# Convolution tiles by group, state steps beside the last convolutions, and decode attention's products on VectorE

## The chip, the cores and the metric

The kernel runs on one core of one Trainium2 chip. The core has TensorE (PE, with its weight loads PEld), VectorE (DVE), ScalarE (ACT), GpSimd (POOL) and SyncE (SP), which here only starts transfers. The metric is the device time of one execution in microseconds. Lower is better.

## What is computed

One step of a decoder of two layers, for a prompt of 1024 tokens and, with the same weights, 8 samples of one token each. All numbers are float32. The first layer (the "even" one) is the one that matters here. Its input projection gives attention's q, k, v and gate, the state-space part's gate z, and the channels xBC with their step dt. Attention's gated output and the state-space part's normalised output go through one output projection. Cut to what the change touches:

```
def even_layer(hn, ...):
    u = hn @ w_in
    q, k, v, g_att, z, xbc, dt_raw = split(u)
    o = dilated attention of the prompt, or, for the samples, of q over cached k, v
    att = o * silu(g_att)
    xbc, new_conv = causal_conv(xbc, conv_buf, conv_w, conv_b)   # 4 taps, then silu
    xs, bm, cm = split(xbc)          # 1024 channels x, 2 x 128 of B, 2 x 128 of C
    dt = softplus(dt_raw + dt_bias); a = -exp(a_log)
    y, new_state = ssd_scan(xs, dt, a, bm, cm, d_skip, ssd_state)
    y = rmsnorm(y * silu(z), ssd_norm_w)
    return concat(att, y) @ w_out

def ssd_scan(...):                   # chunks of 128 tokens, 2 groups of 8 heads
    acum = cumsum(dt * a)            # within a chunk
    decay = exp(acum_i - acum_j), lower triangle
    y_intra = (C B^T * decay * dt) x
    s_local = sum_j B_j exp(last - acum_j) dt_j x_j
    state  <- state * exp(last) + s_local          # from chunk to chunk
    y = y_intra + (C state_before) * exp(acum) + d_skip * x
```

Group 0 of the scan needs B and C of group 0 and channels 0 to 511 of x; group 1 needs the others. The second layer (mLSTM) follows and is not touched.

## The kernel before

**Layout.** Activations lie transposed: 128 channels on the partitions, 1032 tokens (1024 of the prompt, 8 samples) along the free dimension. A product in float32 is made of three reduced-precision products: each operand is split into a high and a low part (`split`, L89), and `mm3` (L103) adds high x high, high x low and low x high. A weight tile of 128 columns by 1024 rows comes with one load, is split by ScalarE (L90) and VectorE (L91), and `Weights` (L115) keeps one split tile ahead. `proj_c` multiplies it with one third of the tokens (344 columns, `c` = 0, 1, 2): 24 matmuls.

**Order of the work.** The program is written as one stream. The builder's scheduler takes that order as a priority: an engine whose next instruction is not ready by the scheduler's own reckoning gets a later one that is. What the engines run is a fixed order per engine, with waits. Tiles come from pools with a fixed number of buffers, and an instruction that writes a new tile waits until the pool has a free one: 15 slabs `S` of 128 x 1040, 3 buffers `EP`, 5 PSUM banks `X` and 3 `MM`, 4 `TMP`.

**First stages.** The input is normalised, and for four pairs of heads q, k, v are projected (to 274 us in the profile). Prompt attention is cut into small pieces in `attq`, which `att_pump` takes out beside the projections: `att_a` (scores; VectorE adds the mask and finds the maximum, L433; ScalarE takes the exponential, L434), `att_b` (VectorE scales P, L468; TensorE transposes it, pT, L470; it is copied, L473 and L475; TensorE multiplies it with v, pO, L487).

**Convolutions** (from 274 us). A loop over 12 weight tiles f: 0 to 7 are x, 8 and 9 are B of groups 0 and 1, 10 and 11 are C. Each has three `conv_c` (the projection; ScalarE copies it out, L242), then `conv_taps` (ScalarE's first tap, L248, and VectorE's three others, L250) and, one tile later, `conv_act` (ScalarE's tanh, L254, and VectorE, L255). Beside tiles 0 to 5 the rest of prompt attention is pumped; beside tiles 4 and later `dpump(1)`, three times per tile, takes a step of `dq`. `dt_prep` (the step sizes, cumulative sums and decays; it stores `acd`) is written behind tile 7.

**Decode attention** is the first part of `dq`: `dec_prep`, eight `dec_k`, `dec_soft`, eight `dec_v`, `dec_fin`. One `dec_k` loads 512 KB of cached keys into an `EP` buffer, POOL multiplies them with q (L634), and VectorE sums (L635). `dec_v` does the same with the values (L651, L652). `dec_fin2` (at gate tile 1) transposes the result on TensorE.

**Gate tiles.** A second loop over 12 weight tiles, `gate_c` each time: 0 to 7 are z, 8 to 11 attention's gate. Beside them run the 16 steps of the state scan, (chunk c, group g), in two halves. `ssd_prep` (`ssd_a`) loads a row of `acd` to all partitions, POOL masks it (L739), ScalarE takes exponentials (L741), TensorE makes C B^T and transposes B and x (pcb, pxt), VectorE multiplies (L747, L758, L759), and ScalarE copies B^T (sbt, L749). `ssd_main` (`ssd_b`) has the products py, pi and psl on TensorE, the state and the results on VectorE (L780 to L789), and one addition on POOL (L791). It runs one step behind the preparation. The order is all chunks, and in each both groups:

```
sq = deque((c, g) for c in range(8) for g in range(2))
own = f < 8 and (c < 2 or f < 2)
```

so tiles 0 and 1 take three steps each and the others two, after one step ahead of the loop. Once per gate tile `dpump` takes one step of the samples' own state update (`dss_step`), in which POOL's products (L839, L841) and VectorE's instructions (L840, L842) alternate. Behind tile 7, `mix_y` multiplies by the gate and normalises; TensorE sums squares there (pst, L188).

Of the kernel before, what the change touches and what calls it, by code (L numbers as in the profile page):

```python
# [28 lines left out]
def body(ctx, tc, I, O):  # L29
# [26 lines left out]
    def S(name, dt=F32):  # L56
        return slab.tile([128, 1040], dt, tag="S", name=name)
# [199 lines left out]
    def conv_raw(raw=None):  # L257
        raw = S("craw") if raw is None else raw
        G.memset(raw[:, 0:3], 0.0)
        return raw  # L260
# [250 lines left out]
    def att_pump(n, limit):  # L511
        for _ in range(n):
            if attq and attq[0][0] < limit:
                attq.popleft()[1]()
# [63 lines left out]
    cur["ep"] = pool("ep0", 3, wstack0)  # L578
    eap = pool("eap", 2, wstack0)

    wq0 = Weights([(I["wf"][f], 1024) for f in range(24)])


    dtb = C("dtb", [128, 16], I["dtb"].partition_broadcast(128))
# [45 lines left out]
    def dec_k(j):  # L630
        t = EP("dk")
        load(t[:, :1024], I["ck"][:, j * 1024 : j * 1024 + 1024])
        tv = t[:, :1024].rearrange("p (a b) -> p a b", b=64)
        G.tensor_tensor(tv, tv, q_b.unsqueeze(1).broadcast_to([128, 16, 64]), mult)  # L634
        V.reduce_sum(dsc[:, j * 16 : j * 16 + 16], tv, AX.X)  # L635

    def dec_soft():
# [9 lines left out]
    def dec_v(j):  # L647
        t = EP("dv")
        load(t[:, :1024], I["cv"][:, j * 1024 : j * 1024 + 1024])
        tv = t[:, :1024].rearrange("p (a b) -> p a b", b=128)  # L650
        G.tensor_tensor(tv, tv, dsc[:, 0:128].unsqueeze(1).broadcast_to([128, 8, 128]), mult)  # L651
        V.reduce_sum(dao[:, j * 8 : j * 8 + 8], tv, AX.X)  # L652

    def dec_fin():
# [39 lines left out]
    scs = C("scs", [128, 12, 3, 8], I["scs"])  # L694
    xbs = C("xbs", [128, 12, 8])
    cvo = C("cvo", [128, 12, 3])
    xbc = []
    later = deque()
    for f in range(12):
        w = wq0.next()  # L700
        raw = conv_raw()
        o = S("cout")
        for c in range(3):
            conv_c(w, xh, xl, c, raw, xbs[:, f])
            if c == 1 and later:
                later.popleft()()
            if f < 6:
                att_pump(3, 4)
            if f > 3:
                dpump(1)  # L710
        conv_taps(raw, o, scw[:, f], scb[:, f : f + 1], cvo[:, f])
        later.append(lambda raw=raw, o=o: conv_act(raw, o))
        xbc.append(o)
        if f == 5:
            att_pump(80, 4)
        if f == 7:
            dt_prep()
    later.popleft()()
    xy, bc = xbc[:8], xbc[8:]
    store(O["sconv"], cvo)  # L720


    st = C("ssdst", [128, 1040])
    ssd_state = {}

    def ssd_prep(c, g):
        tok = slice(c * 128, c * 128 + 128)
        g0 = c * 16 + g * 8
        E = EP("sE")[:, :1024]
        load(E, acd[g0 : g0 + 8, :].rearrange("h i -> (h i)").partition_broadcast(128))  # L730
        Ev = E.rearrange("p (h i) -> p h i", h=8)
        Bt, Ct = bc[g], bc[2 + g]
        ea = None
        if c > 0:
            ea = eap.tile([128, 520], F32, tag="ea", name="ea")[:, :512]
            for u in range(2):
                src = acd[g0 : g0 + 8, :].rearrange("(j u) i -> u j i", u=2)[u]
                load(ea[u * 64 : u * 64 + 64].rearrange("p (j i) -> p j i", j=4), src.partition_broadcast(64))
        G.affine_select(Ev, Ev, [[0, 8], [1, 128]], ALU.is_ge, -1e30, base=0, channel_multiplier=-1)  # L739
        for h in range(8):  # L740
            A.activation(Ev[:, h], Ev[:, h], AF.Exp, bias=nacum[:, g0 + h : g0 + h + 1])  # L741
        if c > 0:
            A.activation(ea, ea, AF.Exp)
        pc = X("pcb")
        PE.matmul(pc[:, 0:128], Bt[:, tok], Ct[:, tok], start=True, stop=True)
        PE.transpose(pc[:, 128:256], Bt[:, tok], ident)
        V.tensor_tensor(Ev, Ev, pc[:, 0:128].unsqueeze(1).broadcast_to([128, 8, 128]), mult)  # L747
        bt = SM("sbt", [128, 128])
        A.copy(bt, pc[:, 128:256])  # L749
        px = X("pxt")  # L750
        for j in range(4):
            PE.transpose(px[:, j * 128 : j * 128 + 128], xy[4 * g + j][:, tok], ident)
        xx = S("sx")
        gi = slice(g0, g0 + 8)
        xd = xx[:, 0:512].rearrange("p (h d) -> p h d", h=8)
        xw = xx[:, 512:1024].rearrange("p (h d) -> p h d", h=8)
        pxv = px.rearrange("p (h d) -> p h d", h=8)
        V.tensor_tensor(xd, pxv, dtf[:, gi].unsqueeze(2).broadcast_to([128, 8, 64]), mult)  # L758
        V.tensor_tensor(xw, pxv, wl[:, gi].unsqueeze(2).broadcast_to([128, 8, 64]), mult)  # L759
        ssd_state[c, g] = (Ev, ea, bt, xx, xd)  # L760

    def ssd_main(c, g):
        tok = slice(c * 128, c * 128 + 128)
        gi = slice(c * 16 + g * 8, c * 16 + g * 8 + 8)
        Ev, ea, bt, xx, xd = ssd_state.pop((c, g))
        py = X("py")
        for j in range(4):
            for hh in range(2):
                h = 2 * j + hh
                o = py[hh * 64 : hh * 64 + 64, j * 128 : j * 128 + 128]  # L770
                PE.matmul(o, xd[:, h], Ev[:, h], start=True, stop=True)
        if c > 0:
            pi = X("pi")
            for j in range(4):
                PE.matmul(pi[:, j * 128 : j * 128 + 128], st[:, g * 512 + j * 128 : g * 512 + j * 128 + 128], bc[2 + g][:, tok], start=True, stop=True)
        pl = X("psl")
        PE.matmul(pl, bt, xx[:, 512:1024], start=True, stop=True)
        sg = st[:, g * 512 : g * 512 + 512]
        if c > 0:
            V.tensor_tensor(ea, pi, ea, mult)  # L780
        if c == 0:
            V.tensor_copy(sg, pl)
        else:
            sv = sg.rearrange("p (h d) -> p h d", h=8)
            V.tensor_tensor(sv, sv, dec[:, gi].unsqueeze(2).broadcast_to([128, 8, 64]), mult)
            V.tensor_tensor(sg, sg, pl, add)
        for j in range(4):
            f = 4 * g + j
            V.scalar_tensor_tensor(xy[f][:, tok], xy[f][:, tok], dsk[:, f : f + 1], py[:, j * 128 : j * 128 + 128], mult, add)  # L789
            if c > 0:  # L790
                G.tensor_tensor(xy[f][:, tok], xy[f][:, tok], ea[:, j * 128 : j * 128 + 128], add)  # L791


    x_b = C("x_b", [128, 64])
# [175 lines left out]
        return get  # L970


    sq = deque((c, g) for c in range(8) for g in range(2))
    pend = deque()

    def ssd_a():
        if sq:
            k = sq.popleft()
            ssd_prep(*k)
            pend.append(k)  # L980

    def ssd_b():
        if len(pend) > 1 or (pend and not sq):
            ssd_main(*pend.popleft())

    def ssd_pump(n=1):
        for _ in range(n):
            ssd_a()
# [5 lines left out]
    for f in range(12):  # L994
        w = wq0.next()
        if f == 1:
            dec_fin2()
        if f == 8:
            ssd_pump(20)
            while pend:  # L1000
                ssd_main(*pend.popleft())
            store(O["ssd"], st[:, :1024])
            mix_y(0, lambda k, u: S("mh", F32R) if u == 0 or k == 0 else EP("ml", F32R))
        if f == 11:
            wqo.fetch()
        for c in range(3):
            t = TMP("gz")
            c0 = c * CH
            if f >= 8:
                a = TMP("al")  # L1010
                n = min(CH, NP - c0)
                load(a[:, :n], ad[f - 8, :, c0 : c0 + n])
                if c == 2:
                    G.tensor_scalar(a[:, n:CH], asamp[:, f - 8], 1.0, None, mult)
            own = f < 8 and (c < 2 or f < 2)
            gate_c(w, xh, xl, c, t[:, :CH], [ssd_a] if own else ())
            if f < 8:
                store(zd[f][:, c0 : c0 + CH], t[:, :CH])
                if own:
                    ssd_b()  # L1020
                if c == 2 and f < 7 or f == 0 and c == 1 or f == 7 and c != 1:
                    dpump(1)
                continue
            if c == 2:
                dpump(1)
            if f % 2 == 0 and c == 0:
                gA.append(S("gA"))
            if c < 2:
                o = (f % 2) * 520 + c0
                n = min(CH, 512 - c0)  # L1030
                V.scalar_tensor_tensor(gA[-1][:, o : o + n], t[:, :n], 0.5, a[:, :n], mult, mult)
            if c > 0:
                n = max(512 - c0, 0)
                V.scalar_tensor_tensor(t[:, n:CH], t[:, n:CH], 0.5, a[:, n:CH], mult, mult)
                store(zd[f][:, c0 + n : c0 + CH], t[:, n:CH])
            bpump(2)
# [827 lines left out]
```

## Time and profile before

| | us |
|---|---|
| median of 3 runs | 2164.42 |
| lowest and highest run | 2162.53, 2165.84 |
| the profiled execution | 2158.71 |
| its span, first to last instruction | 2156.9 |
| TensorE busy | 2097.2 |
| VectorE busy | 1350.3 |
| ScalarE busy | 849.6 |
| POOL busy | 561.9 |

The span is one execution, taken by the hardware profiler. "Busy" is the time in which an engine has at least one instruction running; matmuls are pipelined and their ends are modelled, so a busy TensorE is not one at its peak. The granted clock (PEclk) is the share of full speed that TensorE got; over the whole span its mean is 0.994. An arrow to the left (`<-`) stands between an instruction and what ended its engine's idle time before it. A group of instructions is named by line, engine, operation, and the tiles it writes and reads; "128x1024" is partitions by elements.

### The profile page before, as it was taken

The page shows a single profiled execution, that of the slowest core. Times are in us where ns is not written, and L with a number is a line of the kernel's source. Part 1 is how long each engine was busy: PE and PEld are TensorE (multiplying, and loading weights), DVE is VectorE, ACT ScalarE, POOL GpSimd, SP SyncE. Part 2 cuts the span into 40 slices and gives each one's busy share as a digit, 9 for nine tenths or more (in the row PEclk, how much of TensorE's full clock was granted, in tenths as well). Part 3 has the DMA queues.
Part 4 walks back from the last instruction along what each step waited for, and adds up shares of the span by engine and source line. Part 5 has one row for each costly group of instructions (what it writes and reads, how often), then busy time and mean ns, then how long its engine had stood idle before and what let it go on. Part 6 is the DMA issues. An engine that isn't in the chain of part 4 may idle for free.

```text
span 2156.9 us, 35181 instructions
## 1 busy us (share of the span) xinstructions
PE 2097.2 (97%) x12926; PEld 1880.9 (87%) x12926; DVE 1350.3 (63%) x3176; ACT 849.6 (39%) x1837; POOL 561.9 (26%) x1052
## 2 busy tenths in 40 slices
PE   7999989999999999999999999999999999999998
PEld 6877777997898899989989899898898998987798
DVE  7444388768778655645548566575565665746844
ACT  5434334454425434433425334253343443524421
POOL 4222144015540002142141321413214223141000
PEclk9999999999999999999999999999999999999999
DMA  4222053125555552411214133132231232416852
GB/s 160 72 73 78 26 156 97 47 94 169 184 169 179 178 178 77 99 40 47 89 34 151 44 97 116 37 115 78 84 131 29 92 106 68 142 30 199 280 169 94
DMA packets 162076, 232.29 MB, mean 108 GB/s; under 512 B 41200, under 2 KB 106976, under 8 KB 161904
## 3 DMA queue, kind: packets, MB, share of 16 engines
q1 hardware_dynamic: 161904, 230.04, 34.0%
q8 instruction: 102, 1.67, 0.3%
q14 instruction: 70, 0.57, 0.1%
HBM read 174.35 MB, written 55.62 MB: 107 GB/s over the span
## 4 chain that ended last, share of the span: by engine, by line
PE 78%; DVE 7%; DMA 3%; POOL 3%; issue 2%; ACT 2%; POOLq 0%; SPq 0%; DVEq 0%; ACTq 0%
PE pf L112 32%; PE pvo L112 16%; PE po L931 14%; PE pq L112 4%; PE mN L112 2%; PE mC L112 2%; PE pS L428 1%; PE pO L487 1%; PE mS L1294 1%; PE pT L470 1%; DMA sE<-acd 1%; POOL mCl L91 1%; DVE P L468 1%; PE mH L1355 1%; PE mS L1296 1%
## 5 line engine op out<-in xcount | busy, mean ns | idle before, releaser
L112 PE MATMUL pf<-yh,wh 128*128 128x344 f32 x1152 | 370.1, 321 | 0.0
L112 PE MATMUL pf<-yl,wh 128*128 128x344 f32 x1152 | 368.9, 320 | 0.0
L112 PE MATMUL pf<-yh,wl 128*128 128x344 f32 x1152 | 368.5, 320 | 0.0
L91 DVE TENSOR_TENSOR wl<-raw,wh 128x1024 fp32r<-128x1024 f32 x128 | 161.7, 1263 | 156.3 <-ACT wh L90 155.7
L90 ACT CAST wh<-raw 128x1024 fp32r<-128x1024 f32 x128 | 133.9, 1047 | 254.8 <-PE pf L112 93.6
L112 PEld LDWEIGHTS pf<-yh,wh 128*128 128x128 f32 x1152 | 216.9, 188 | 1.3 <-ACT craw L242 1.0
L112 PEld LDWEIGHTS pf<-yl,wh 128*128 128x128 f32 x1152 | 216.5, 188 | 0.0
L112 PEld LDWEIGHTS pf<-yh,wl 128*128 128x128 f32 x1152 | 216.4, 188 | 0.0
L112 PE MATMUL pvo<-wvh,yh 128*128 128x512 f32 x512 | 206.0, 402 | 0.0
L112 PE MATMUL pvo<-wvh,yl 128*128 128x512 f32 x512 | 201.9, 394 | 0.0
L112 PE MATMUL pvo<-wvl,yh 128*128 128x512 f32 x512 | 201.7, 394 | 0.0
L112 PE MATMUL pf<-xh,wh 128*128 128x344 f32 x576 | 195.4, 339 | 0.8 <-ACT gth L236 0.8
L112 PE MATMUL pf<-xh,wl 128*128 128x344 f32 x576 | 188.0, 326 | 0.0
L112 PE MATMUL pf<-xl,wh 128*128 128x344 f32 x576 | 187.9, 326 | 0.0
L1282 DVE TENSOR_SCALAR mx<-mx,mbs,md 128x256 f32<-128x256 f32 x64 | 26.4, 413 | 176.7 <-POOL md L1281 176.7
L250 DVE SCALAR_TENSOR_TENSOR cout<-craw,mcw,cout 128x1024 f32<-128x1024 f32 x96 | 123.1, 1284 | 13.4 <-ACT cout L248 11.9
L931 PE MATMUL po<-oh,wl 128*128 128x512 f32 (+2 forms) x384 | 122.9, 320 | 1.6 <-DVE wl L91 1.6
L931 PE MATMUL po<-oh,wh 128*128 128x512 f32 (+2 forms) x384 | 123.0, 321 | 0.9 <-ACT oh L90 0.9
L931 PE MATMUL po<-ol,wh 128*128 128x512 f32 (+2 forms) x384 | 123.0, 321 | 0.0
L112 PEld LDWEIGHTS pf<-xh,wh 128*128 128x128 f32 x576 | 110.5, 192 | 7.6 <-issue 5.9
L112 PEld LDWEIGHTS pvo<-wvh,yl 128*128 128x128 f32 x512 | 96.1, 188 | 22.3
L112 PEld LDWEIGHTS pf<-xl,wh 128*128 128x128 f32 x576 | 110.7, 192 | 4.3 <-issue 4.3
(440 smaller groups left out, 5030.3 us busy)
## 6 DMA issues: line engine op xcount, KB each, us to landing
raw<-in_wo SPq DMA_DIRECT2D x56, 512.0 KB
raw<-in_wq SPq DMA_DIRECT2D x32, 512.0 KB
raw<-in_wvo SPq DMA_DIRECT2D x32, 512.0 KB
dC<-in_mcs SPq DMA_DIRECT2D x32, 512.0 KB
out_mcs<-dC SPq DMA_DIRECT2D x32, 512.0 KB
raw<-in_wf SPq DMA_DIRECT2D x24, 512.0 KB
sE<-acd SPq DMA_DIRECT2D x16, 512.0 KB
raw<-in_wz SPq DMA_DIRECT2D x16, 512.0 KB
```

The source lines that it names most:

```text
L90: A.copy(hi, src)
L91: eng.tensor_tensor(lo, src, hi.bitcast(F32), sub)
L112: PE.matmul(out, l, r, start=i == 0, stop=i == n - 1)
L250: V.scalar_tensor_tensor(o[:, :NP], raw[:, j : j + NP], w4[:, j : j + 1], o[:, :NP], mult, add)
L428: PE.matmul(p[:, :n], qT[g][hs, qs], kT[g][hs, ks], start=True, stop=True)
L468: V.tensor_scalar(P, P, u["f"][:, kind, x, h : h + 1], None, mult)
L470: PE.transpose(pt[:, h * n + k : h * n + k + 128], P[:, k : k + 128], ident)
L487: PE.matmul(po[h * 64 : h * 64 + 64, qs], v, PT[:, h * n + k * 128 : h * n + k * 128 + 128], start=j + k == 0, stop=j == 7 and k == nk - 1)
L931: PE.matmul(p[:, :m], wt[:, ws], at, start=i == 0 and q == 0, stop=i == nk - 1 and q == 2)
L1282: V.tensor_scalar(x, x, bs[:, 6:7], d[:, 2:3], sub, mult)
L1294: PE.matmul(pS[:, 0:128], hd["k"][j][:, tok], hd["q"][j][:, tok], start=j == 0, stop=j == 1)
L1296: PE.transpose(pS[:, 128 + j * 128 : 256 + j * 128], hd["k"][j][:, tok], ident)
```

## The change

The convolution tiles come in the order B and C of group 0, x of group 0, part of it before the two tiles of group 1's B and C, then the rest of x. The tiles are kept in a dictionary by number. The queue of state steps takes group 0's first four chunks, then group 1's, then the later chunks alternately. The functions `ssd_prep`, `ssd_main`, `ssd_a` and `ssd_b` are the same and stand ahead of the convolution loop; beside each of its last four tiles one `ssd_a` and one `ssd_b` are called. `dt_prep` comes behind the sixth tile of the loop. Decode attention is pumped beside tiles number 5 to 10 of the loop, with what is left of it behind the last. The gate tiles take 11 steps after the one ahead of them, so 12 with it. The products of `dec_k` and `dec_v` are on VectorE.

```
+    conv_order = [8, 10, 0, 1, 2, 3, 9, 11, 4, 5, 6, 7]
+    wq0 = Weights([(I["wf"][f], 1024) for f in conv_order + list(range(12, 24))])
...
-        G.tensor_tensor(tv, tv, q_b.unsqueeze(1).broadcast_to([128, 16, 64]), mult)
+        V.tensor_tensor(tv, tv, q_b.unsqueeze(1).broadcast_to([128, 16, 64]), mult)
...
-        G.tensor_tensor(tv, tv, dsc[:, 0:128].unsqueeze(1).broadcast_to([128, 8, 128]), mult)
+        V.tensor_tensor(tv, tv, dsc[:, 0:128].unsqueeze(1).broadcast_to([128, 8, 128]), mult)
...
-    for f in range(12):
...
-            if f < 6:
-                att_pump(3, 4)
-            if f > 3:
-                dpump(1)
...
-        if f == 5:
-            att_pump(80, 4)
-        if f == 7:
-            dt_prep()
...
+    sq = deque([(c, g) for g in range(2) for c in range(4)] + [(c, g) for c in range(4, 8) for g in range(2)])
...
+    for i, f in enumerate(conv_order):
+        w = wq0.next()
+        raw = conv_raw()
+        o = S("cout")
+        for c in range(3):
+            conv_c(w, xh, xl, c, raw, xbs[:, f])
+            if c == 1 and later:
+                later.popleft()()
+            if i < 6:
+                att_pump(3, 4)
+            if 4 < i < 11:
+                dpump(1)
+            if i > 7 and c > 0:
+                (ssd_a if c == 1 else ssd_b)()
+        conv_taps(raw, o, scw[:, f], scb[:, f : f + 1], cvo[:, f])
+        later.append(lambda raw=raw, o=o: conv_act(raw, o))
+        xbc[f] = o
+        if i == 5:
+            att_pump(80, 4)
+            dt_prep()
+    later.popleft()()
+    xy, bc = [xbc[f] for f in range(8)], [xbc[f] for f in range(8, 12)]
+    dpump(40)
...
-            own = f < 8 and (c < 2 or f < 2)
+            own = f < 8 and (c == 0 or c == 1 and f in (1, 3, 5))
...
-                if own:
+                if own or f == 7:
                     ssd_b()
```

More of the change, by code (lines that the diff above doesn't have):

```diff
@@ L579, in body @@
     eap = pool("eap", 2, wstack0)
-    wq0 = Weights([(I["wf"][f], 1024) for f in range(24)])
+    conv_order = [8, 10, 0, 1, 2, 3, 9, 11, 4, 5, 6, 7]
+    wq0 = Weights([(I["wf"][f], 1024) for f in conv_order + list(range(12, 24))])
     dtb = C("dtb", [128, 16], I["dtb"].partition_broadcast(128))
@@ L696, in body @@
     cvo = C("cvo", [128, 12, 3])
-    xbc = []
+    xbc = {}
     later = deque()
-    for f in range(12):
[L700 to L706, printed above, removed]
-            if f < 6:
-                att_pump(3, 4)
-            if f > 3:
-                dpump(1)
-        conv_taps(raw, o, scw[:, f], scb[:, f : f + 1], cvo[:, f])
-        later.append(lambda raw=raw, o=o: conv_act(raw, o))
-        xbc.append(o)
-        if f == 5:
-            att_pump(80, 4)
-        if f == 7:
-            dt_prep()
-    later.popleft()()
-    xy, bc = xbc[:8], xbc[8:]
-    store(O["sconv"], cvo)
     st = C("ssdst", [128, 1040])
@@ L731, in ssd_prep @@
         Ev = E.rearrange("p (h i) -> p h i", h=8)
-        Bt, Ct = bc[g], bc[2 + g]
+        Bt, Ct = xbc[8 + g], xbc[10 + g]
         ea = None
@@ L751, in ssd_prep @@
         for j in range(4):
-            PE.transpose(px[:, j * 128 : j * 128 + 128], xy[4 * g + j][:, tok], ident)
+            PE.transpose(px[:, j * 128 : j * 128 + 128], xbc[4 * g + j][:, tok], ident)
         xx = S("sx")
@@ L774, in ssd_main @@
             for j in range(4):
-                PE.matmul(pi[:, j * 128 : j * 128 + 128], st[:, g * 512 + j * 128 : g * 512 + j * 128 + 128], bc[2 + g][:, tok], start=True, stop=True)
+                PE.matmul(pi[:, j * 128 : j * 128 + 128], st[:, g * 512 + j * 128 : g * 512 + j * 128 + 128], xbc[10 + g][:, tok], start=True, stop=True)
         pl = X("psl")
@@ L788, in ssd_main, with ssd_a, ssd_b @@
             f = 4 * g + j
-            V.scalar_tensor_tensor(xy[f][:, tok], xy[f][:, tok], dsk[:, f : f + 1], py[:, j * 128 : j * 128 + 128], mult, add)
+            V.scalar_tensor_tensor(xbc[f][:, tok], xbc[f][:, tok], dsk[:, f : f + 1], py[:, j * 128 : j * 128 + 128], mult, add)
             if c > 0:
-                G.tensor_tensor(xy[f][:, tok], xy[f][:, tok], ea[:, j * 128 : j * 128 + 128], add)
+                G.tensor_tensor(xbc[f][:, tok], xbc[f][:, tok], ea[:, j * 128 : j * 128 + 128], add)
+    sq = deque([(c, g) for g in range(2) for c in range(4)] + [(c, g) for c in range(4, 8) for g in range(2)])
+    pend = deque()
+    def ssd_a():
+        if sq:
+            k = sq.popleft()
+            ssd_prep(*k)
+            pend.append(k)
+    def ssd_b():
+        if len(pend) > 1 or (pend and not sq):
+            ssd_main(*pend.popleft())
+    for i, f in enumerate(conv_order):
[21 more added lines that the diff above has]
+    dpump(40)
+    store(O["sconv"], cvo)
     x_b = C("x_b", [128, 64])
@@ L970, in wstream @@
         return get
[L973 to L984, printed above, removed]
     def ssd_pump(n=1):
```

## The prediction

> **What bounds the kernel now.** I read the head of the profile page first, then the chain that ended last.
>
> ```profile
> PE 2097.2 (97%) x12926; PEld 1880.9 (87%) x12926; DVE 1350.3 (63%) x3176; ACT 849.6 (39%) x1837; POOL 561.9 (26%) x1052
> PE 78%; DVE 7%; DMA 3%; POOL 3%; issue 2%; ACT 2%; POOLq 0%; SPq 0%; DVEq 0%; ACTq 0%
> ```
>
> TensorE is busy for 97% of the span and carries 78% of the chain. The change adds no matmul and takes none away. So it can win only time in which TensorE stands still or runs at a lower granted clock inside the two stages that it touches, and lose only by making more of it. I therefore asked for the busy time of each engine by stretch: convolutions beside attention (274 to 392), the other convolutions (392 to 470), gate tiles with state steps (470 to 600), and what is left of the gate stage. Columns: stretch, its length, busy time and instructions of PE, PEld, DVE, ACT, POOL, then the granted clock, the DMA share and GB/s.
>
> ```profile
> 274.00:392.00 118.00, 107.86 (x690) 89.72 (x690) 101.85 (x199) 47.80 (x122) 47.10 (x27) 0.94 0.36 106
> 392.00:470.00 78.00, 78.00 (x500) 78.00 (x499) 47.06 (x54) 38.21 (x77) 10.24 (x15) 1.00 0.25 79
> 470.00:520.00 50.00, 48.26 (x357) 41.57 (x355) 46.20 (x82) 24.34 (x67) 16.79 (x22) 1.00 0.42 141
> 520.00:600.00 80.00, 72.42 (x516) 63.78 (x517) 65.77 (x113) 37.13 (x107) 46.20 (x56) 0.98 0.55 174
> 600.00:660.00 60.00, 57.45 (x381) 54.62 (x379) 44.78 (x77) 19.81 (x39) 22.82 (x25) 1.00 0.57 183
> ```
>
> The first stretch loses 118 - 107.86 = 10.1 us idle and 0.06 x 118 = 7.1 us of clock: 17.2 us. The second loses nothing and leaves VectorE 78 - 47.06 = 30.9 us free. From 470 to 600 the loss is 1.7 + 7.6 us idle and 0.02 x 80 = 1.6 us of clock: 10.9 us. These 28.1 us are the ceiling of what the change can win. Next, what ended TensorE's idle time from 265 to 670 (total us, times, longest):
>
> ```profile
> PE pcb L745 <- ACT sbt L749: 5.6, 5, 1.8
> PE pO L487 <- DVE PT L475: 5.2, 2, 3.8
> PE pxt L752 <- DVE sx L759: 3.7, 3, 1.7
> PE pT L470 <- DVE P L468: 2.8, 2, 2.6
> PE pst L188 <- DVE yac L217: 2.0, 1, 2.0
> PE pS L428 <- DVE ast L433: 1.9, 1, 1.9
> ```
>
> The attention rows (pO, pT, pS: 5.2 + 2.8 + 1.9 = 9.9 us) all name VectorE, and so does pxt of the state step. pcb + pxt = 9.3 us is the idle time of the gate tiles. The pst row belongs to the normalisation behind them, which is not changed.
>
> **Why VectorE is late there.** The groups of the first stretch, POOL's two products and VectorE's main groups, and one VectorE row from 392 to 470 for comparison (it comes last). Columns: busy us, mean ns, idle time before and what ended it.
>
> ```profile
> L651 POOL TENSOR_TENSOR dv<-dv,dsc 128x1024 f32<-128x1024 f32 x8 | 23.1, 2904 | 23.7 <-DMA dv<-in_cv 13.9 <-DVE aft L455 6.1 <-ACT dsc L645 3.7
> L634 POOL TENSOR_TENSOR dk<-dk,q_b 128x1024 f32<-128x1024 f32 x8 | 21.8, 2731 | 23.6 <-DMA dk<-in_ck 8.9 <-DMA q_b<-qd 8.6 <-DVE dsc L635 6.0
> L250 DVE SCALAR_TENSOR_TENSOR cout<-craw,scw,cout 128x1024 f32<-128x1024 f32 x15 | 26.8, 1788 | 1.2 <-ACT cout L248 1.2
> L468 DVE TENSOR_SCALAR P<-P,aft 128x256 f32<-128x256 f32 x38 | 14.8, 456 | 0.1
> L468 DVE TENSOR_SCALAR P<-P,aft 128x128 f32<-128x128 f32 x10 | 6.5, 693 | 0.0
> L635 DVE TENSOR_REDUCE dsc<-dk 128x16 f32<-128x1024 f32 x8 | 9.6, 1207 | 2.5 <-POOL dk L634 2.5
> L250 DVE SCALAR_TENSOR_TENSOR cout<-craw,scw,cout 128x1024 f32<-128x1024 f32 x19 | 25.2, 1329 | 2.4 <-ACT cout L248 2.0
> ```
>
> While POOL multiplies for decode attention (23.1 + 21.8 = 44.9 us of this stretch), the same tap instruction takes VectorE 1.788 us instead of 1.329: 15 x 0.459 = 6.9 us. The scaling of P is stretched too; its row over the whole run gives a minimum of 270 and a median of 342 ns for both widths together, and the second row says when the first products run:
>
> ```profile
> L468 DVE TENSOR_SCALAR P<-P,aft x128: 270/342/2511, 92.4 to 386.5; 128x256 f32<-128x256 f32 x88, 128x128 f32<-128x128 f32 x40
> L634 POOL TENSOR_TENSOR dk<-dk,q_b x8: 2349/2393/3375, 282.7 to 318.2; 128x1024 f32<-128x1024 f32 x8
> ```
>
> That is 38 x (0.456 - 0.342) = 4.3 and 10 x (0.693 - 0.270) = 4.2 us more. Together 15.4 us of VectorE's 101.85 are stretching; I count none for the other instructions, so this is a low value. All four attention stalls are waits for such an instruction or for one queued behind it.
>
> The second row also shows that the place in the source is only a priority. The pump starts at tile 4, so behind 4 x 3 x 24 = 288 matmuls of tiles 0 to 3; at 78.00/500 = 0.156 us that is at least 45 us after 274, or 319. The last dk product starts at 318.2: the builder's scheduler takes ready work forward to wherever the engine is free. I assume that it does the same with the products on VectorE.
>
> **Decode products on VectorE (L635, L652).** They leave POOL with their 44.9 us, and the stretching goes: -15.4 us on VectorE. They add 16 instructions of 128x1024. The nearest row is L747 below, a product of the same size with one operand in PSUM: 16 x 1.214 = 19.4 us. Upper bound: the same size under load, L250's 1.788, gives 28.6 us; lower bound: the reduction of the same size, 1.207, gives 19.3. I take 19.4, since POOL falls silent there. VectorE then needs 101.85 - 15.4 + 19.4 = 105.9 us where TensorE needs 118 - 17.2 = 100.8 us. So VectorE would itself bound the stretch at about 106, less what slips behind 392 into the 30.9 free us. I add 2 us for latencies: 107.8, and the stretch gains 10.2 us, with 0 and 17.2 as bounds. In front of a product stands its load on VectorE's own queue now; that is the first rival.
>
> How much of the loss is clock, by slices of 4 us around two stalls:
>
> ```profile
> 286.00:290.00 4.00, 0.66 (x5) 0.38 (x3) 4.00 (x10) 0.46 (x2) 2.23 (x1) 1.00 0.00 0
> 290.00:294.00 4.00, 3.49 (x17) 3.17 (x18) 3.96 (x12) 0.63 (x4) 0.00 (x0) 0.57 0.36 31
> 298.00:302.00 4.00, 2.63 (x26) 2.02 (x22) 4.00 (x4) 1.17 (x2) 4.00 (x4) 0.84 0.45 168
> 302.00:306.00 4.00, 4.00 (x23) 3.62 (x19) 4.00 (x3) 0.00 (x0) 3.91 (x3) 0.74 0.71 200
> ```
>
> The 3.8 us stall is followed by a clock of 0.57, and 1.37 us of idleness in 298 to 302 by 0.84 and 0.74: short stalls cost clock here as well, so removing them returns both. The Trainium skill (TensorE: Matmul & The Clock Gate, "Why this matters for your kernels") tells us to avoid idle gaps above about 3 us, since one idle window takes the clock down. By that rule only the one long stall costs clock (4 x 0.43 = 1.7 us), and as an estimate the other 5.4 of the 7.1 us would stay when the short stalls go; at the forecast's share of 10.2 in 17.2 that is 3.2 us less, or 2153. The trace does not bear this out (0.74 after 1.37 us), and I go by the trace.
>
> **Four state steps to the last convolutions, twelve to the gates.** What one step costs VectorE, and the sample's state step beside it (470 to 625):
>
> ```profile
> L747 DVE TENSOR_TENSOR sE<-sE,pcb 128x1024 f32<-128x1024 f32 x16 | 19.4, 1214 | 2.7 <-PE pcb L746 2.7
> L789 DVE SCALAR_TENSOR_TENSOR cout<-cout,dsk,py 128x128 f32<-128x128 f32 x64 | 19.1, 343 | 0.0
> L758 DVE TENSOR_TENSOR sx<-pxt,dtr 128x512 f32<-128x512 f32 x16 | 10.9, 683 | 0.0
> L840 DVE SCALAR_TENSOR_TENSOR dst<-dst,dsc,dso 128x512 f32<-128x512 f32 x12 | 13.1, 1131 | 4.2 <-POOL dso L839 4.2
> L842 DVE TENSOR_REDUCE y_b<-dso 128x4 f32<-128x512 f32 x12 | 8.2, 683 | 7.1 <-POOL dso L841 7.1
> ```
>
> A step is 1.21 + 4 x 0.343 + 5 x 0.683 (L758, L759, L780, L785, L786 have one size) = 6.0 us of VectorE. Its matmuls, ScalarE's exponentials and the acd loads move with it and are as many as before.
>
> In the tail, four preparations and three completed steps put at most 4 x 6.0 = 24 us on VectorE, into 30.9 free us, in a stretch that grows by the steps' own matmuls. They fit. But each preparation is a chain (acd load, POOL's mask, ScalarE, VectorE, TensorE), and a convolution waits behind it. One such wait in the gates is at most 1.8 us (pcb) and one 1.7 (pxt). The bounds are 0 and 3 x 1.8 = 5.4 us; I take a loss of 1.5, as VectorE has slack there. At the last convolution 12 results, 2 raw tiles and 2 step tiles ask for 16 slabs of 15: the step waits for one activation that is next on its queue anyway, and I count nothing. If that activation is late, it costs up to the 1.8 us above.
>
> In the gates, the pcb and pxt stalls come once per tile for five tiles. VectorE waits in order for POOL's products of the sample's state step (4.2 + 7.1 = 11.3 us in these rows), the step's L747 queues behind them, and the next pcb finds its buffer held. Before, each of these tiles has a second step right behind the first; afterwards only three of the eight tiles have two. Three stalls in place of five keep 10.9 x 3/5 = 6.5 us; four fewer steps take 24 us off VectorE, which would pull that towards 2. I take 5 us kept, a gain of 5.9, with bounds of 0 and 8.9.
>
> Edits counted at nothing: the order of the weight loads (same 24 loads, each fetched one tile ahead); the decay preparation after the sixth tile rather than the eighth (six small matmuls on a queue that has them either way; the first acd load needs it before the ninth tile; if it is late, it is a preparation's wait as above); the end of decode attention behind the convolutions, whose result TensorE transposes at gate tile 1, one tile of 3 x 24 x 0.156 = 11.2 us later. If its two small round trips through memory take longer, that tile waits for the rest, a few us.
>
> **Sum.** -10.2 (attention stretch) + 1.5 (tail) - 5.9 (gates) = -14.6 us. The profiled execution took 2158.71 us (span 2156.9), 5.7 below the median of the runs, 2164.42. On its own scale the result is 2144.1; against the median it is 2164.4 - 14.6 = 2149.8 us.
>
> **Rivals.** First, slower: loads at the head of VectorE's queue. POOL waited 13.9 + 8.9 + 8.6 = 31.4 us for loads, with nothing behind it. On VectorE the mask, scaling and taps of attention stand behind each such wait, and TensorE behind those. If more than 14.6 of these 31.4 us arrive there, the gain is gone; all of them give 2149.8 + 31.4 = 2181. For it: three buffers, one load queue in order. Against it: POOL waited because it was idle; a VectorE busy for 101.85 of 118 us comes to each product later, when the load has landed. Chance 0.13.
>
> Second, no change: VectorE is full, and the stalls only change their names. With products at 1.788 us VectorE needs 101.85 - 15.4 + 28.6 = 115.1 us in the first stretch, which with the 2 us then gains 1; with half the gate gain (3.0) and the tail's 1.5 the time is 2164.4 - 2.5 = 2161.9. It is also the case in which the scheduler puts the products where attention needs VectorE. Chance 0.14.
>
> Third: the gate stalls stay whole, since they come from the sample's state step, which is not changed. Then 2149.8 + 5.9 = 2155.7. For it: L840 and L842 name POOL. Chance 0.18.
>
> **How the numbers follow.** The forecast has 0.55; its own range is 2145 to 2157: a tail at 0 with gates at 8.9 gives 2164.4 - 19.1 = 2145.3, a first stretch that gains 3 us less with a tail of 5.4 gives 2164.4 - 7.7 = 2156.7. If every bound falls well, 17.2 + 8.9 = 26.1 gives 2138. The range over the cases is 2139 to 2164: it takes in the second and third rivals and leaves out the first. A measurement of this kernel can tell about 0.2%, 4.3 us. Faster by more: the forecast and the third rival, 0.73. The same: 0.14. Slower: 0.13.
>
> **What would show it.** Right: no POOL product for dk and dv; L250 beside attention near 1.33 us; from 274 to the end of attention about 10 us less with a clock near 1.00; VectorE 95% busy there; state steps before the first gate tile; fewer pcb waits for sbt. Wrong: VectorE waiting for loads of ck or cv for more than 15 us in all; TensorE idle in the last four convolutions by more than 5 us; gate tiles that stall as often as before.

## The result and the profile after

| | before | changed |
|---|---|---|
| median, us | 2164.03 (6 runs, 2162.53 to 2165.88) | 2153.08 (6 runs, 2151.57 to 2154.99) |
| profiled execution, us | 2158.71 | 2152.76 |
| ratio of the runs | | 0.995, 95% interval 0.9939 to 0.996 |

The change makes the kernel 11 us faster, where 14.6 were forecast. The two profiled executions are only 5.95 us apart: the one of before was 5.3 us below the median of its runs. All medians in this document are of fast runs; two executions of e2, below, of 4084 and 7125 us were slow and are left out.

The head of the page of the changed kernel:

```profile
PE 2094.5 (97%) x12926; PEld 1880.2 (87%) x12926; DVE 1351.5 (63%) x3192; ACT 849.9 (40%) x1837; POOL 524.7 (24%) x1036
```

The matmuls are as many as before. VectorE has the 16 products more (3192 instructions against 3176) and yet the same busy time, 1351.5 against 1350.3 us: what it gained in work it lost in stretching.

By stretch (columns as in the prediction: length, busy time of PE, PEld, DVE, ACT, POOL, granted clock, DMA share, GB/s). Attention's last matmul now starts at 373 us, not at 391, so the stretches are cut elsewhere:

```profile
274.00:374.00 100.00, 99.78 (x685) 82.86 (x685) 82.55 (x192) 47.60 (x121) 3.39 (x10) 1.00 0.32 93
374.00:463.00 89.00, 89.00 (x601) 86.88 (x600) 75.54 (x92) 43.98 (x98) 17.76 (x21) 1.00 0.39 120
463.00:473.00 10.00, 6.56 (x36) 5.06 (x36) 9.59 (x21) 5.19 (x15) 4.66 (x6) 0.73 0.43 117
473.00:520.00 47.00, 43.20 (x304) 38.25 (x302) 37.59 (x67) 21.38 (x58) 19.59 (x23) 0.99 0.46 140
520.00:600.00 80.00, 74.29 (x503) 67.59 (x502) 62.18 (x100) 33.14 (x90) 41.40 (x48) 0.96 0.54 178
600.00:645.00 45.00, 45.00 (x303) 43.04 (x303) 33.82 (x60) 13.48 (x27) 18.33 (x21) 1.00 0.47 152
645.00:680.00 35.00, 29.61 (x179) 29.26 (x178) 29.90 (x66) 17.61 (x33) 2.95 (x4) 0.85 0.59 174
```

The first row is the success: 0.2 us idle and a clock of 1.00, where before had 10.1 us and 0.94. The third row is new: at the end of the convolutions TensorE stands still for 3.4 us and the clock falls to 0.73. The gate tiles (rows 4 and 5) lose 3.8 + 5.7 = 9.5 us idle, as much as the 9.3 of before, and their clock is lower (0.99 and 0.96, against 1.00 and 0.98). The last row loses 5.4 us, at a clock of 0.85. For the same place before, the end of the gate tiles:

```profile
650.00:686.00 36.00, 33.37 (x210) 32.78 (x209) 29.88 (x65) 18.89 (x36) 3.56 (x5) 0.95 0.52 163
```

That was 2.6 us idle, at a clock of 0.95. The waits of TensorE in the changed kernel, 265 to 680 us (total, times, longest), say what is late in each place:

```profile
PE pst L188 <- DVE yac L217: 5.4, 1, 5.4
PE pcb L722 <- ACT sbt L726: 4.3, 2, 3.1
PE py L748 <- DVE ea L757: 2.7, 1, 2.7
PE psl L754 <- DVE cout L766: 1.5, 1, 1.5
PE pi L752 <- DVE ssdst L763: 1.4, 1, 1.4
PE pxt L729 <- DVE sx L736: 1.4, 2, 1.0
```

pO, pT and pS of attention are gone from the list. py, psl and pi are new, and pst is longer. From the first convolution matmul to the first of the output projection it is 273.81 to 679.73 = 405.9 us, against 274.13 to 686.34 = 412.2 before: 6.3 us, which is all of the difference between the two profiled executions.

### The profile page after: what moved, and what is told of

Read it like the earlier page. It is cut to its first block, busy times and chain, and to the rows that moved or that the text cites. A ratio compares the mean times of both kernels' runs of the same rounds, so it can differ in the third digit from the quotient of the medians.

```text
span 2151.0 us, 35161 instructions
## 1 busy us (share of the span) xinstructions
PE 2094.5 (97%) x12926; PEld 1880.2 (87%) x12926; DVE 1351.5 (63%) x3192; ACT 849.9 (40%) x1837; POOL 524.7 (24%) x1036
## 3 DMA queue, kind: packets, MB, share of 16 engines
q8 instruction: 102, 1.67, 0.3%
## 4 chain that ended last, share of the span: by engine, by line
PE 64%; DVE 2%; DMA 2%; POOL 1%; ACT 1%; issue 1%; POOLq 0%; DVEq 0%; SPq 0%; ACTq 0%
PE pf L112 26%; PE pvo L112 16%; PE po L947 14%; PE mN L112 2%; PE mC L112 2%; PE mS L1297 1%; DMA dC<-in_mcs 1%; POOL mCl L91 1%; PE mH L1358 1%; PE mS L1299 1%; DMA mE<-mud 1%; PE prb L207 0%; PE pst L188 0%; DVE dC L1420 0%; POOL md L1283 0%
## 5 line engine op out<-in xcount | busy, mean ns | idle before, releaser
L112 PEld LDWEIGHTS pvo<-wvh,yh 128*128 128x128 f32 x512 | 96.2, 188 | 21.0 <-issue 1.3
```

The costliest lines, as they stand in the source:

```text
L112: PE.matmul(out, l, r, start=i == 0, stop=i == n - 1)
```

## Experiments

All compare with runs of the kernel before on the same chip. The medians of before in the three groups of runs were 2164.39, 2163.25 and 2164.92 us. "Products alone" below is e1; "the changed kernel" is the one of this document.

### e1: products alone

The kernel before, and of the diff only this, and the same in `dec_v`:

```
-        G.tensor_tensor(tv, tv, q_b.unsqueeze(1).broadcast_to([128, 16, 64]), mult)
+        V.tensor_tensor(tv, tv, q_b.unsqueeze(1).broadcast_to([128, 16, 64]), mult)
```

> The kernel before with decode attention's 16 products on VectorE and nothing else. My theory (POOL's products stretched VectorE's instructions beside attention, and TensorE waited for those): 8 to 14 us faster than before, ratio 0.9935 to 0.9963; no TensorE stall over 1 us beside attention; the gate tiles lose about 11 us as before. Rival (the regrouped state steps carry the gain): 0 to 3 us faster, ratio 0.9985 to 1.000.

Measured: 2147.13 us median, ratio 0.9916 (0.9902 to 0.9929). That is more than I expected, and 6 us faster than the changed kernel, whose interval begins at 0.9939. TensorE's waits, 265 to 680:

```profile
PE pcb L745 <- ACT sbt L749: 7.3, 4, 3.6
PE pxt L752 <- DVE sx L759: 3.7, 3, 1.7
PE pst L188 <- DVE yac L217: 1.9, 1, 1.9
```

No wait of attention is left but one of 0.2 us; the gate tiles wait 7.3 + 3.7 = 11.0 us as expected. So two lines of the diff bring more than the whole of it, and the rest of the diff costs.

### e2: regrouping alone

The changed kernel with both products back on POOL.

> The changed kernel with decode attention's products back on POOL: the new order of tiles and state steps alone. My theory: within 3 us of before, ratio 0.9985 to 1.0015, since the stalls beside attention (about 10 us idle) stay and the gate tiles gain nothing that the wait before pst does not take. Rival (the regrouped steps carry the gain): 6 to 11 us faster, ratio 0.995 to 0.997.

Measured: 2173.22 us, ratio 1.0041 (1.0026 to 1.0055), slower than either theory said. The row of the tap instruction on VectorE from 274 to 392, and TensorE's waits:

```profile
L250 DVE SCALAR_TENSOR_TENSOR cout<-craw,scw,cout 128x1024 f32<-128x1024 f32 x15 | 25.3, 1689 | 2.5 <-ACT cout L248 2.3
```

```profile
PE pcb L722 <- ACT sbt L726: 14.4, 3, 9.7
PE pst L188 <- DVE yac L217: 5.0, 1, 5.0
```

The stretching is there (1.689 us), and a single pcb wait of 9.7 us has come, at the border to the gates. There ScalarE stood 5.7 us waiting for a load of `acd` (the exponential of `ea`, L720), and the last convolution's activation and the copy that TensorE waited for came behind it on its queue. With the products on POOL the regrouping is a loss of about 9 us.

### e3: POOL kept busy for nothing

The changed kernel, and in each decode step, for a result that nobody reads (a half of the state's tile, filled with ones before and written over later); `dec_v` has the same with `dsc`:

```
+        jv = st[:, 512:1024].rearrange("p (a b) -> p a b", b=64)
+        for _ in range(2):
+            G.tensor_tensor(jv, jv, q_b.unsqueeze(1).broadcast_to([128, 8, 64]), mult)
         V.reduce_sum(dsc[:, j * 16 : j * 16 + 16], tv, AX.X)
```

> The changed kernel, in which POOL in addition multiplies 128x512 elements twice beside each decode step into a place that nobody reads: as much POOL work as the removed products, with no engine waiting for it. Theory that contention stretched VectorE: the tap instruction L250 beside attention is back near 1.7 us, and the time is 4 to 12 us above the changed kernel, ratio to before 0.997 to 1.001. Rival (VectorE's wait in order for POOL's result was the cost): L250 at 1.28 us and the time of the changed kernel, ratio 0.994 to 0.996.

Measured: 2182.2 us, ratio 1.0075 (1.0062 to 1.0088): 29 us above the changed kernel, where 4 to 12 were expected, though no engine waits for this work. VectorE's groups, 274 to 374 us, of this kernel and then of the changed one:

```profile
L250 DVE SCALAR_TENSOR_TENSOR cout<-craw,scw,cout 128x1024 f32<-128x1024 f32 x12 | 19.5, 1621 | 0.6 <-ACT cout L248 0.5
L468 DVE TENSOR_SCALAR P<-P,aft 128x256 f32<-128x256 f32 x22 | 17.8, 875 | 0.0
```

```profile
L250 DVE SCALAR_TENSOR_TENSOR cout<-craw,scw,cout 128x1024 f32<-128x1024 f32 x14 | 17.9, 1280 | 1.2 <-ACT cout L248 1.1
L468 DVE TENSOR_SCALAR P<-P,aft 128x256 f32<-128x256 f32 x38 | 10.6, 347 | 0.1
```

The scaling of P, one input from the tile and one number per partition, takes 0.875 us instead of 0.347 while POOL multiplies; the taps, with two inputs, 1.621 instead of 1.280. TensorE then waits for attention again:

```profile
PE pO L487 <- DVE PT L475: 11.0, 2, 9.3
PE pT L470 <- DVE P L468: 8.1, 2, 7.4
```

This shows that POOL's work as such stretches VectorE beside attention, and that this alone brings the stalls back. It does not measure the rival's share: in the trace before, VectorE also waited 2.5 + 2.0 = 4.5 us for POOL's results there. Why e3 costs more than the products did is not shown. Its 32 multiplications run in two rows, from 282 to 311 and from 361 to 388 us, and take POOL 49.0 us, against the 44.9 before; VectorE now has the decode products beside them.

### e4: the kernel before, once more

> The kernel before once more, for a second trace of it: its profiled execution was 5 us below the median of its runs. If the stalls are fixed by the order of the instructions, the same waits appear at the same places with lengths within 1 us, and the time lies between 2158 and 2166. If they depend on the execution, waits appear elsewhere or differ by more than 2 us in all.

Measured: 2162.36 us for the one execution.

```profile
PE pO L487 <- DVE PT L475: 5.0, 2, 3.8
PE pT L470 <- DVE P L468: 4.6, 2, 4.3
PE pS L428 <- DVE ast L433: 1.8, 1, 1.8
```

The same waits stand at the same places; the longest pT wait is 4.3 us where it was 2.6. So the places are fixed by the order of the instructions, and the lengths move by up to 2 us, more than the 1 us expected. The waits do not explain why the first trace was 5 us below its runs: from 265 to 680 us they add up to 22.0 us there and to 22.6 us here. The mean granted clock differs: 0.994 in the first trace, 0.991 in this one and 0.988 to 0.992 in the eleven runs beside it. As an estimate, 0.003 of the 2097 us in which TensorE is busy is 6.3 us, which covers the 3.7 us between the two executions. The first trace was lucky in its clock.

### e5, e6, e7: three tries at the new waits

e5 takes the fourth step out of the tail:

```
-            if i > 7 and c > 0:
+            if 7 < i < 11 and c > 0:
...
-            own = f < 8 and (c == 0 or c == 1 and f in (1, 3, 5))
+            own = f < 8 and (c == 0 or c == 1 and f in (1, 3, 5, 6))
```

> The changed kernel with state steps beside the third-, second- and next-to-last of the convolutions only (three preparations instead of four), and one step more in gate tile 6. Theory that the wait around 465 us in the changed kernel (3.4 us idle, then a lower clock, 6 us in all) is the fourth step, which at the last convolution asks for a 16th of 15 slabs: that wait is gone, and the time is 3 to 6 us below the changed kernel, ratio to before 0.992 to 0.9935. Rival (the end of decode attention on VectorE stands in front): the wait stays, ratio 0.9945 to 0.9955.

Measured: 2150.16 us, ratio 0.9943 (0.9923 to 0.9963). The timeline of TensorE, 464 to 480 us, rows with a wait (in brackets):

```profile
468.29 0.49 PE L722 MATMUL pcb<-cout 128*128 128x128 f32 x2 [1.05 <-ACT sbt L726]
...
474.58 1.16 PE L752 MATMUL pi<-cout,ssdst 128*128 128x128 f32 x8 [1.86 <-DVE ssdst L763]
477.87 0.33 PE L729 MATMUL pxt<-ident,cout 128*128 128x128 f32 x1 [1.67 <-DVE cout L255]
```

The wait for py is gone, but 1.05 + 0.40 + 1.86 + 1.67 = 5.0 us of others stand a few us later (the 0.40 is a pxt wait between them). The time does not tell the theories apart, and the 16th slab is not shown to be the cause.

e6 ends the steps one gate tile earlier:

```
-            own = f < 8 and (c == 0 or c == 1 and f in (1, 3, 5))
+            own = f < 7 and (c == 0 or c == 1 and f in (1, 3, 5, 6))
...
-                if own or f == 7:
+                if own or f == 6:
```

> The changed kernel with its 11 steps of the gate loop in tiles 0 to 6 (two in tiles 1, 3, 5 and 6, none in 7). Theory that the 5.4 us before pst come because the last state step now lies in tile 7, so that the gate's loads and sums behind it start late: the wait before pst falls to 2 us or less, and the time is 2 to 6 us below the changed kernel, ratio 0.992 to 0.994. Rival (the chain behind the steps is as long wherever they end, and TensorE only arrives earlier): the wait stays above 4 us, ratio 0.9945 to 0.996.

Measured: 2153.34 us, ratio 0.9956 (0.9943 to 0.9969), no gain.

```profile
PE pcb L722 <- ACT sbt L726: 4.5, 4, 3.1
PE pst L188 <- DVE yac L217: 2.8, 1, 2.8
PE py L748 <- DVE ea L757: 2.7, 1, 2.7
```

The wait before pst is halved (2.8 against 5.4), which lies between the two expectations. pst starts no earlier, at 653.4 us against 652.3 in the changed kernel, but this execution was 3.2 us behind already at the py wait (471.5 against 468.4). Counted from there, the chain behind the last step ends 2.1 us earlier, so the late last step is part of the wait. The median does not follow.

e7 writes the end of decode attention later (without `dpump(40)` behind the convolutions, with one `dpump` at gate tile 0, `dec_fin2` at tile 2).

> The changed kernel with the end of decode attention written at gate tile 0 and its transposition at gate tile 2, not behind the convolutions and at tile 1. Theory of the 16th slab: the wait around 465 us stays above 2.5 us, the time is within 2 us of the changed kernel. Rival (the short VectorE chain that ends decode attention is in front of what py waits for): the wait falls below 1 us, the time is 3 to 6 us lower, ratio 0.992 to 0.9935.

Measured: 2152.02 us, ratio 0.995 (0.9931 to 0.997).

```profile
467.35 0.52 PE L729 MATMUL pxt<-ident,cout 128*128 128x128 f32 x3 [1.01 <-DVE de L660]
470.62 1.97 PE L748 MATMUL py<-sE,sx 128*64 128x128 f32 x16 [2.74 <-DVE ea L757]
```

L660 is the end of decode attention, and it still runs before the transposition: the scheduler took it forward to where it had been. The edit did not move what it was to move, and tells nothing. What exactly delays the step at the border stays open. In the changed kernel it is VectorE's queue, in which the activation of a convolution (which itself waited 2.2 us for ScalarE), that chain of 1.6 us and a weight split stand ahead of what py waits for.

### e8: the sample's products on VectorE as well, without regrouping

```
-            G.tensor_tensor(ov, xd[:, 4 * u : 4 * u + 4]..., mult)
+            V.tensor_tensor(ov, xd[:, 4 * u : 4 * u + 4]..., mult)
...
-            G.tensor_tensor(ov, tv, C_b..., mult)
+            V.tensor_tensor(ov, tv, C_b..., mult)
```

> The kernel before with decode attention's products on VectorE and the two products of the sample's state step on VectorE as well; no regrouping. Theory that the gate tiles' stalls come from VectorE waiting in order for POOL in that step: the pcb and pxt waits (11 us idle with products alone) fall below 5 us and the time is 4 to 10 us below products alone, ratio to before 0.987 to 0.990. Rival (VectorE is full there): no gain or a loss, ratio 0.9915 to 0.997.

Measured: 2148.34 us, ratio 0.993 (0.991 to 0.995), nothing against products alone. The stretch 520 to 600 us, then TensorE's waits:

```profile
520.00:600.00 80.00, 69.52 (x463) 61.26 (x462) 62.84 (x105) 29.66 (x83) 24.98 (x32) 0.91 0.49 151
```

```profile
PE pcb L745 <- ACT sbt L749: 11.3, 5, 3.5
```

The wait before pst is gone, and pcb's has grown from 7.3 to 11.3 us. With two state steps per tile the exchange brings nothing. The rival's reason for that, a full VectorE, is not what the row shows: it is busy for 62.84 of 80 us. The longest pcb wait (3.5 us, at 567 us) ends with ScalarE's copy of B^T, which came behind exponentials on ScalarE's queue; the first of these had waited 1.97 us for its load of `acd`.

### e9: the new order without the moved steps

The changed kernel, with `sq` and `own` as before and without the calls beside the last four convolutions.

> The changed kernel with its order of convolution tiles, its places for decode attention and its products on VectorE, but with all 16 state steps back in the gate tiles in the old order and pace. Theory that the moved steps are what costs the 7 us between the changed kernel and products alone: the time of products alone, ratio to before 0.9905 to 0.993, TensorE idle under 1 us from 455 to 475. Rival (the later place of decode attention, whose products run on to 450 us, costs it): the time of the changed kernel, ratio 0.9945 to 0.996.

Measured: 2147.29 us, ratio 0.9921 (0.9906 to 0.9937), the time of products alone. From 455 to 475 us:

```profile
455.00:475.00 20.00, 20.00 (x143) 18.27 (x143) 18.93 (x31) 10.47 (x29) 2.48 (x3) 1.00 0.30 101
```

No idle time. So neither the order of the tiles nor the later place of decode attention costs anything that the runs can tell: it is the moved steps, with their new order and pace, that cost about 6 us, as long as POOL makes the sample's products.

### e10: the changed kernel with the sample's products on VectorE

The edit of e8 on the changed kernel.

> The changed kernel with the two products of the sample's state step on VectorE too. Theory that the gate tiles stall because VectorE waits in order for POOL, and that the moved steps leave VectorE room for these products: gate waits fall from 9.5 us to under 4 us, the wait before pst falls too, and the time is 5 to 10 us below the changed kernel, ratio to before 0.990 to 0.993. Rival (the stalls are VectorE's load, whoever multiplies): 2 us or less either way, ratio 0.994 to 0.997.

Measured: 2137.15 us, ratio 0.9872 (0.9855 to 0.9889): 16 us below the changed kernel, where 5 to 10 were expected, and 11 below e8.

```profile
520.00:600.00 80.00, 77.30 (x543) 71.03 (x542) 74.60 (x133) 35.62 (x94) 20.36 (x34) 1.00 0.60 192
```

```profile
PE py L748 <- DVE ea L757: 2.7, 1, 2.7
PE pcb L722 <- ACT sbt L726: 2.7, 2, 2.1
PE pss L825 <- DVE dst L824: 1.6, 1, 1.6
```

The gate tiles lose 2.7 us in this stretch instead of 5.7, with VectorE at 74.6 of 80, and the wait before pst is gone. What POOL had cost VectorE in the sample's step stands in two rows of the changed kernel, 470 to 640 us:

```profile
L856 DVE SCALAR_TENSOR_TENSOR dst<-dst,dsc,dso 128x512 f32<-128x512 f32 x16 | 17.7, 1133 | 7.0 <-POOL dso L855 7.0
L858 DVE TENSOR_REDUCE y_b<-dso 128x4 f32<-128x512 f32 x16 | 10.9, 679 | 7.4 <-POOL dso L857 7.4
```

In e10 both idle times are 0.0, and L856 takes 0.807 us instead of 1.133. So waiting (14.4 us) and stretching (16 x 0.326 = 5.2 us) went together, and so did the load on POOL's own queue, where the state scan's mask and addition stand too; no run separates the three. Why the products on VectorE pay with the regrouped steps and not in e8 is not shown either; lack of room on VectorE is not the reason (62.84 of 80 us busy in e8, 74.6 here).

### e11: no arithmetic in the sample's step

The changed kernel; the sample's state is loaded and stored unchanged, and its output `y_b` is set to zero.

> The changed kernel without the arithmetic of the sample's own state step: its state is loaded and stored unchanged, and its output is set to zero. Theory (the third rival of the prediction: the gate tiles stall because this step holds VectorE): TensorE's waits from 480 to 600 us, 9.5 us idle in the changed kernel, fall below 2 us, and the time is 8 to 16 us below the changed kernel. Rival (the state scan's own chain of POOL, ScalarE, VectorE and TensorE stalls it): at least 5 us of pcb, pxt, pi or psl waits stay, and the time falls by less than 6 us.

Measured: 2135.39 us, ratio 0.986 (0.984 to 0.9879), 17.7 us below the changed kernel, somewhat more than the theory said.

```profile
520.00:600.00 80.00, 80.00 (x572) 74.61 (x572) 46.77 (x87) 34.59 (x94) 21.38 (x34) 1.00 0.54 183
```

Not a moment of idleness, in the stretch where the changed kernel loses 5.7 us and some clock. From 480 to 520 us one wait of 1.4 us is left. This shows that, with the regrouped steps, the sample's step is the cause of the gate tiles' waits. It also narrows the cause: e10 keeps that work, all of it on VectorE, and is only 1.8 us slower, with overlapping intervals. So it is POOL's part in the step that costs, not the work as such.

### e12: one of the sample's two products, without regrouping

Products alone, with only the second of the two edits of e8.

> The kernel before with decode attention's products on VectorE and the second product of the sample's state step, with C, on VectorE as well; the first stays on POOL. Theory that half of the sample's products on VectorE removes one of the two waits for POOL without filling VectorE: gate waits under 8 us (12 with products alone, 12 with both moved) and 2 to 5 us below products alone, ratio to before 0.989 to 0.991. Rival (any of them moved only exchanges a wait for load): the time of products alone within 2 us, ratio 0.991 to 0.9935.

Measured: 2138.55 us, ratio 0.9877 (0.9859 to 0.9894), 8.6 us below products alone: more than expected.

```profile
L840 DVE SCALAR_TENSOR_TENSOR dst<-dst,dsc,dso 128x512 f32<-128x512 f32 x16 | 18.2, 1178 | 9.6 <-POOL dso L839 9.6
L841 DVE TENSOR_TENSOR dso<-dst,BC_b 128x512 f32<-128x512 f32 x16 | 12.0, 790 | 0.0
```

```profile
PE pcb L745 <- ACT sbt L749: 5.1, 5, 1.3
PE pst L188 <- DVE yac L217: 0.8, 1, 0.8
```

One wait for POOL is left on VectorE (9.6 us) and the other is gone; pcb's longest wait is 1.3 us, down from 3.6. VectorE is busy for 74.6 of the 80 us from 520 to 600 us, as in e10, with two steps per tile. Of the versions that compute everything e10 and e12 are the fastest, and their intervals overlap.

| sample's products on | two steps per tile, none in the tail | regrouped steps |
|---|---|---|
| POOL, both | 0.9916 (e1), 0.9921 (e9) | 0.995 (the change) |
| POOL, first only | 0.9877 (e12) | not tried |
| VectorE, both | 0.993 (e8) | 0.9872 (e10) |

## Why the prediction was right, and where its steps failed

**The bound, and the reason in the attention stretch: right.** POOL's products stretched VectorE, and TensorE waited: e3 brings both back with work that nobody waits for, and e1 gains 17 us from the products alone. The price of a product was 1.214 us; it is 1.218 for dk and 1.222 for dv:

```profile
L652 DVE TENSOR_TENSOR dv<-dv,dsc 128x1024 f32<-128x1024 f32 x8 | 9.8, 1222 | 7.0 <-DMA dv<-in_cv 6.4 <-ACT dsc L646 0.6
L635 DVE TENSOR_TENSOR dk<-dk,q_b 128x1024 f32<-128x1024 f32 x8 | 9.5, 1218 | 0.0
```

**The size there: too small.** The forecast left 7 of the 17.2 us, since VectorE "would itself bound the stretch at about 106". It did not: the last dv product starts at 447.3 us, far behind attention, and VectorE is busy for 82.6 of the 100 us, not for 95%. I had allowed for work that slips behind 392 and then did not count it. The idle time fell to 0.2 us.

**The tail: +1.5 forecast, 3.4 us idle and a clock of 0.73 measured.** The idle time lies within the bounds of 0 to 5.4; with the missing clock, by the prediction's own measure 0.27 x 10 = 2.7 us, it is 6.1 and does not. The longest wait, 2.7 us for py, is longer than the 1.8 that the gates' rows gave. What stood ahead of it on VectorE are an activation and the end of decode attention, which the prediction had counted at nothing. In e5, with the fourth step moved to the gates, other waits came in its place.

**The gates: the step that failed.** "Three stalls in place of five" was to gain 5.9 us. The idle time went from 9.3 to 9.5 us. The pcb waits did become fewer, two in place of five, as forecast, but they are longer (3.1 and 1.2 us), and psl, pi and pss have waits of 3.8 us that were not there. I counted the occasions on which a second step follows the first, and the cause lies in the sample's state step: e11, without its arithmetic, has 1.4 us of waits there. The third rival, which had 0.18, named this and was right for the gates; its time, 2155.7, is 2.6 us from the median, nearer than the forecast's 2149.8.

**What the sum left out:** the wait before pst, which I had called unchanged. It grew from 2.0 to 5.4 us, and the clock around it fell from 0.95 to 0.85. The last state step, now in gate tile 7, is part of it (e6: 2.8 us when the steps end one tile earlier), but not alone: in e10 the steps end in the same tile and the wait is gone, so POOL's products for the sample stand behind this wait as well. With the gates' missing 5.9 us and the tail's excess, this takes back more than the extra gain in the attention stretch.

So -14.6 us became -11.0 in the medians, and the forecast's own range, 2145 to 2157, holds 2153.1, by errors in both directions: about 7 us too little in the first stretch (17.2 against 10.2) and, as the remainder, about 11 too much behind it (6 lost against 4.4 gained). That they nearly cancel is luck. The direction, and the reason for the gain, are not.

**The first rival** was there and small: VectorE waited 6.4 us for loads of cv, in three places, where 14.6 would have undone the gain. No TensorE wait in attention followed from it. **The second** is refuted by the first row of the stretches: VectorE was not full. **The rule of the Trainium skill on idle gaps** (TensorE: Matmul & The Clock Gate, "Why this matters for your kernels"), as the prediction applied it, would have left most of the missing clock in the attention stretch. The clock there is 1.00, and 0.98 or more in every experiment with the products on VectorE but e3, so the traces do not agree; that its time, 2153, is the measured one is chance.

## What to carry to other kernels

Elementwise work on POOL beside a VectorE that feeds TensorE was not free here, even where nobody waited for its result (29 us in e3): compare the duration of one VectorE instruction with and without POOL at work, and price the move by that. A diff with two independent parts should be timed in parts; here two lines gave 17 us and the other part took 6 back, until a third move turned that part into a gain of 11 (e10 against e8); e12 comes within 1.4 us of e10 without that part. Before spreading the visible victims of a stall (the state steps) over more tiles, remove the suspected culprit (the sample's step) for one run: that run shows whether it is the cause.

## What the runs showed of the hardware

POOL's work does not stretch all of VectorE's instructions alike. In e3, 274 to 374 us, the scaling of P goes from 0.347 to 0.875 us (a factor of 2.5) and the taps from 1.280 to 1.621 (1.3); the reduction of dk, 128x1024, stays at 1.21, and the pass over the scores in PSUM (L433) at 0.420. Where POOL multiplies without a break, 12 times in 16.2 us from 282 us on, nine scalings of P take 12.05 us: 1.34 us each, as long as one multiplication (1.35).

The granted clock falls in places where the profile shows no idle time of TensorE (whose ends are modelled). In e12, for instance, two neighbouring slices beside attention, and then the same two in e1, which writes attention in the same order:

```profile
340.00:345.00 5.00, 5.00 (x18) 3.21 (x17) 2.82 (x9) 0.60 (x2) 0.00 (x0) 0.80 0.00 0
345.00:350.00 5.00, 5.00 (x30) 3.39 (x29) 2.07 (x10) 3.44 (x12) 0.00 (x0) 0.86 0.00 0
```

```profile
340.00:345.00 5.00, 5.00 (x23) 3.22 (x23) 2.82 (x9) 1.27 (x5) 0.00 (x0) 1.00 0.00 0
345.00:350.00 5.00, 5.00 (x34) 3.80 (x31) 3.62 (x11) 2.67 (x11) 0.00 (x0) 1.00 0.00 0
```

TensorE is busy for all 10 us in both, and the clock is 0.80 and 0.86 in e12 and 1.00 in e1. Nor does a short wait settle it. The 1.37 us beside attention in before were followed by 0.74, and waits of 1.25 and 0.99 us in the changed kernel's gates (at 578 and 580 us) by 0.57. But 1.69 us in the gates of before (at 508 us) were followed by 1.00 in the next 4 us, and so were 2.17 us in e9 (at 493 us) in the next 5. So the prediction's reading that short stalls cost clock holds in some places only; I cannot say what decides.
